# Seven buffers instead of four for the experts' weights, and half blocks loaded two row blocks to a buffer

## The chip, the cores and the metric

The kernel runs on one core of one Trainium2 chip. The metric is the device time of one execution in microseconds (us); the time before is 2666.2 us, the median of 3 runs (2665.56 to 2667.45). Everything is float32.

## What is computed

Three transformer blocks run one after the other on a sequence of 256 tokens of width 1024. Nearly all of the change's effect lies in the mixture of experts that ends the second block. Cut to what matters:

```python
N_EXPERTS, TOP_K, D_EXPERT = 8, 2, 3584        # D_MODEL = 1024, 256 tokens

def swiglu(x, w_in, w_out):
    gate, up = jnp.split(x @ w_in, 2, axis=-1)
    return (jax.nn.silu(gate) * up) @ w_out

def moe_swiglu(x, w_router, w_in, w_out):      # w_in [8, 1024, 7168], w_out [8, 3584, 1024]
    xt = x.reshape(b * s, d)
    logits = (xt @ w_router).astype(jnp.float32)
    top_val, top_idx = lax.top_k(logits, TOP_K)
    top_w = jax.nn.softmax(top_val, axis=-1)
    gates = jnp.sum(jax.nn.one_hot(top_idx, N_EXPERTS) * top_w[..., None], axis=1)
    y = jnp.zeros_like(xt)
    for e in range(N_EXPERTS):
        y = y + gates[:, e:e + 1] * swiglu(xt, w_in[e], w_out[e])
    return y.reshape(b, s, d)
```

An expert has 29.4 MB of `w_in` and 14.7 MB of `w_out`, the eight together 352 MB, and every byte is read once.

## The kernel before

The program is written with tiles from pools. A scheduler turns it into one fixed order of instructions for each engine and adds the waits; on the chip every engine takes its instructions in that order. A tile takes a free buffer of its pool, and whoever writes a buffer anew waits until the last reader of the tile before has done. Two pools matter here, both with buffers of 8 KB in each of the 128 partitions, which is 1 MB: `raw` with 4 buffers, which holds weights as they come from memory, and `big` with 12 buffers (tag `u8`, taken through `K.u8`), which holds activations and operands.

The mixture of experts is in `moe`. The tokens of each expert are picked with matmuls, in groups of 32 tokens: the experts are ranked by how many tokens they got, five have room for 96 tokens (3 groups) and three for 64 (2 groups). They run in four pairs, `PAIRS = [(0, 5), (1, 6), (2, 7), (3, 4)]`; the document calls them pairs 0 to 3. In pairs 0 to 2 a 96-token expert goes with a 64-token one, in pair 3 both have 96. Each expert of a pair is a generator (`run`, and in it `expert`), and the two are stepped in turn, a piece of weights each, after the first of the pair has had `LEAD = 4` pieces alone. The first accumulates in the PSUM pool `mm`, the second in `ps`, so `mm<-wr` and `ps<-wr` tell the two apart in the profile.

In `expert` the hidden width 3584 goes in blocks of 1024: three full blocks and a half block of 512. In the first expert, the first 512 are computed otherwise (`dense`, all tokens, through `linear`), so it has three full blocks and no half block. For a block of `w` columns, 8 row blocks of `w_in` come one after the other (128 rows, gate and up: 1 MB for a full block, 512 KB for a half one), each in a `wr` tile of `raw` (L964 to L966). For each group of tokens four matmuls read the piece (L969), each with 32 columns of weights (the tokens) and the piece as moving data. After the eighth, `silu` and the product are made (L977, L978), and two pieces later `flush` turns the result with transposes (L947) into the tiles `eh` (L949), which lie in `big`. Then 14 pieces of `w_out`, 256 rows and 1 MB each, come into `wr` (L985, L986) and are read by L990. At the end the groups are joined (L1178, L1180), split, and added to the result with the matmuls at L1189.

All loads of weights are issued by SyncE (SP), in the order of the program. SP waits there, with everything behind it, until the `raw` buffer of the next piece is free:

```python
self.raw = pool("raw", 4)
...
raw = k.raw.tile([128, 2048], F32, name="wr")[:, :2 * w].rearrange("p (g n) -> p g n", g=2)
src = w_in[c * 128:c * 128 + 128].rearrange("p (g n) -> p g n", g=2)[:, :, c0:c0 + w]
k.mark = nc.sync.dma_start(raw, src)
```

While the experts run, `big` holds the result `moe_y`, the tokens `xth` and `xtl`, the picked tokens `xg` of the pair and from its second block on those of the next, and two tiles `eh` for each of the two experts: nine buffers of twelve.

Of the kernel before, what the change touches and what calls it, by code (L numbers as in the profile page):

```python
# [10 lines left out]
F32 = mybir.dt.float32  # L11
# [13 lines left out]
class K:  # L25


    def __init__(self, tc, ctx, inp):
        self.tc, self.nc, self.inp = tc, tc.nc, inp
        pool = lambda name, bufs, **kw: ctx.enter_context(tc.tile_pool(name=name, bufs=bufs, **kw))  # L30
        self.raw = pool("raw", 4)
        self.wh = pool("wh", 4)
        self.wl = pool("wl", 4)
        self.big = pool("big", 12)
        self.work = pool("work", 1)
        self.small = pool("small", 3)
        self.const = pool("const", 1)
        self.mm = pool("mm", 3, space=PSUM)
        self.ps = pool("ps", 5, space=PSUM)
        self.consts = {}  # L40
        self.mark = None
        self.pend = []

    def const_in(self, name, queue=None):
        if name not in self.consts:
            src = self.inp["c_" + name]
            t = self.const.tile(list(src.shape), F32, name="c_" + name)
            if queue is not None:
                queue.dma_start(t, src)
            else:  # L50
                self.load(t, src)
            self.consts[name] = t
        return self.consts[name]
# [869 lines left out]
def expert(k, pool, xg, o, cap, w_in, w_out, hidden, evac, first=None, midway=None):  # L923

    nc = k.nc
    ident = k.const_in("ident")
    groups = cap // 32  # L930
    n = hidden // 128
    hs = [k.u8(F32, "eh")[:, :16 * cap].rearrange("p (c t) -> p c t", c=16) for _ in range(2)]
    half = 12 if first else 16
    hidden_units = lambda c, m=1: hs[c >= half][:, c - half * (c >= half):c - half * (c >= half) + m]
    if first:
        first(hidden_units(0, 4))

    def accumulators():
        name = "mm" if pool is k.mm else "ps"
        return [pool.tile([128, 512], F32, name=name) for _ in range(groups)]  # L940

    def turn(g, h, c0, sub):

        m = sub // 128
        p = k.ps.tile([128, m, 64], F32, name="ps")
        for c in range(m):
            nc.tensor.transpose(p[:, c], h[0:64, c * 128:c * 128 + 128], ident[0:64, 0:64])  # L947
        dst = hidden_units(c0 // 128, 2 * m)[:, :, g * 32:g * 32 + 32].rearrange("p (s c) t -> p c s t", s=2)
        nc.vector.tensor_copy(dst, p.rearrange("p c (s t) -> p c s t", s=2))  # L949

    pend = []

    def flush():
        for f in pend:
            f()
        pend.clear()

    starts = list(range(512 if first else 0, hidden, 1024))
    for c0 in starts:
        w = min(1024, hidden - c0)  # L960
        sub = w // 2
        acc = accumulators()
        for c in range(8):
            raw = k.raw.tile([128, 2048], F32, name="wr")[:, :2 * w].rearrange("p (g n) -> p g n", g=2)  # L964
            src = w_in[c * 128:c * 128 + 128].rearrange("p (g n) -> p g n", g=2)[:, :, c0:c0 + w]
            k.mark = nc.sync.dma_start(raw, src)  # L966
            for g in range(groups):
                for j in range(4):
                    nc.tensor.matmul(acc[g][32 * j:32 * j + 32, :sub], xg[:, c, o + 32 * g:o + 32 * g + 32],  # L969
                                     raw[:, j // 2, j % 2 * sub:j % 2 * sub + sub], start=(c == 0), stop=(c == 7),  # L970
                                     tile_position=(0, 32 * j), skip_group_check=True)
            if c == 1:
                flush()
            if c == 7:
                for g in range(groups):
                    h = k.wl.tile([128, 1024], F32, name="wl")[:, :512]
                    nc.scalar.activation(h[64:128, :sub], acc[g][0:64, :sub], AF.Silu)  # L977
                    nc.vector.tensor_tensor(h[0:64, :sub], h[64:128, :sub], acc[g][64:128, :sub], op=OP.mult)  # L978
                    pend.append(partial(turn, g, h, c0, sub))
                if midway and c0 == starts[1]:  # L980
                    midway()
            yield
    acc = accumulators()
    for i in range(0, n, 2):
        raw = k.raw.tile([128, 2048], F32, name="wr").rearrange("p (g n) -> p g n", g=2)  # L985
        k.mark = nc.sync.dma_start(raw, w_out[i * 128:i * 128 + 256].rearrange("(g p) n -> p g n", p=128))  # L986
        for g in range(groups):
            for j in range(4):
                c = i + j // 2
                nc.tensor.matmul(acc[g][32 * j:32 * j + 32], hidden_units(c)[:, 0, 32 * g:32 * g + 32],  # L990
                                 raw[:, j // 2, j % 2 * 512:j % 2 * 512 + 512], start=(i == 0), stop=(i == n - 2),
                                 tile_position=(0, 32 * j), skip_group_check=True)
        if i == 2:
            flush()
        if i < n - 2:
            yield
    for g in range(groups):
        evac(g, acc[g])
    yield


def moe(k, x, xs, w_router, w_in, w_out, y, before_rest):
# [167 lines left out]
    def run(pool, xg, o, cap, wi, wo, pt, g, last, first=None, midway=None):  # L1170
        made = []

        def evac(i, p):
            if not made:
                made.append(k.w(4, [2, 512], F32, "res"))
            res = made[0]
            odd = k.wh.tile([128, 1024], F32, name="wh")[:, :512]
            nc.scalar.copy(odd[:64], p[64:128])  # L1178
            for c in range(2):
                nc.vector.tensor_tensor(res[32 * i:32 * i + 32, c], odd[32 * c:32 * c + 32], p[32 * c:32 * c + 32], op=OP.add)  # L1180

        yield from expert(k, pool, xg, o, cap, wi, wo, hidden, evac, first, midway)
        f = [v.tile([128, 1024], F32R, name=m).rearrange("p (c n) -> p c n", c=2) for v, m in ((k.wh, "wh"), (k.wl, "wl"))]
        k.split(f[0][:cap], f[1][:cap], made[0][:cap])
        for c in range(2):
            for t in range(2):
                q = k.ps.tile([128, 512], F32, name="ps")
                for i in range(2):
                    nc.tensor.matmul(q, pt[:cap, t], f[i][:cap, c], start=(i == 0), stop=(i == 1))  # L1189
                o = slice(c * 512, c * 512 + 512)  # L1190
                nc.vector.scalar_tensor_tensor(y[:, t, o], q, g(t), y[:, t, o], op0=OP.mult, op1=OP.add)
                if last:
                    nc.vector.bn_stats(stats[:, t, c], y[:, t, o])
# [456 lines left out]
```

## Time and profile before

| what | us |
|---|---|
| time, median of 3 runs | 2666.2 |
| the profiled execution's own time | 2663.86 |
| its span (first to last instruction in the trace) | 2662.1 |
| granted TensorE clock over the span | 0.981 |
| PE busy (94% of the span) | 2509.5 |
| DVE busy (45%) | 1187.8 |
| ACT busy (32%) | 855.5 |

The experts' pieces are issued from 1386 us on, and the last matmuls on them end at 2383 us. In the page's 40 slices (66.6 us each) the DMA engines are busy 80% of the time or more from 1464 to 2329 us and move 321 to 401 GB/s there, against 55 to 269 GB/s in the slices before. So the kernel has two regimes: a first one in which DVE and ACT prepare the weights for PE and the DMA has time to spare, and the experts, in which DVE and ACT hardly work, and PE and the DMA are both near their limits. An engine's busy time is the time covered by its instructions; a matmul's end is modelled, so that the last one before a pause counts about 0.2 us more than its slot in a dense row.

### The profile page before, as it was taken

How to read it: one execution, taken by the hardware profiler on the slowest of the kernel's cores; microseconds unless marked ns; L12 is line 12 of the kernel's file. 1: busy time of each engine (PE TensorE's matmuls, PEld its weight loads, DVE VectorE, ACT ScalarE, POOL GpSimd, SP SyncE). 2: the span in 40 equal slices, each digit the busy share in tenths (PEclk: the TensorE clock that was granted, in tenths of full speed). 3: DMA queues.
4: the chain of work that ended last, by engine and by line, in shares of the span. 5: the costliest groups of instructions: out<-in, count | busy, mean ns of one | idle time of the engine just before them, and what ended most of it. 6: DMA issues, size and time to landing. Idle time of an engine off the chain costs nothing. (4 is left out here: it accounts for less than half of the span.)

```text
span 2662.1 us, 40466 instructions
## 1 busy us (share of the span) xinstructions
PE 2509.5 (94%) x16925; PEld 1655.0 (62%) x16925; DVE 1187.8 (45%) x1932; ACT 855.5 (32%) x1291; POOL 60.6 (2%) x82
## 2 busy tenths in 40 slices
PE   8999999999999999999999988988898899888999
PEld 7888888878787887787974322232223233326777
DVE  4555758775555566655472102110211111128665
ACT  4434445444443334443561000000110000005553
POOL 0000000000000000000000000000000000002100
PEclk9999989999999999999999999999999999998999
DMA  7555514453556854556527999999899989877513
GB/s 254 178 173 185 173 55 162 161 188 127 191 181 207 213 174 158 185 185 201 161 96 269 384 358 354 401 339 389 334 375 335 397 340 371 321 289 236 196 64 111
DMA packets 254398, 630.46 MB, mean 237 GB/s; under 512 B 21359, under 2 KB 40064, under 8 KB 253952
## 3 DMA queue, kind: packets, MB, share of 16 engines
q1 hardware_dynamic: 252000, 624.57, 65.3%
q10 hardware_dynamic: 2208, 3.21, 0.9%
q8 instruction: 136, 2.23, 0.3%
q14 instruction: 54, 0.44, 0.0%
HBM read 623.55 MB, written 4.19 MB: 236 GB/s over the span
## 5 line engine op out<-in xcount | busy, mean ns | idle before, releaser
L93 DVE TENSOR_TENSOR wl<-wr,wh 128x1024 fp32r<-128x1024 f32 x494 | 595.0, 1212 | 381.3 <-ACT wh L92 362.8
L92 ACT CAST wh<-wr 128x1024 fp32r<-128x1024 f32 x494 | 512.2, 1044 | 512.8 <-PE mm L164 376.1
L161 PE MATMUL mm<-wh,xh 128*128 128x512 f32 (+2 forms) x1264 | 491.2, 389 | 9.0 <-ACT xh L92 6.4
L164 PE MATMUL mm<-wh,xl 128*128 128x512 f32 (+2 forms) x1264 | 487.1, 386 | 5.9 <-DVE xl L93 5.9
L162 PE MATMUL mm<-wl,xh 128*128 128x512 f32 (+2 forms) x1264 | 485.6, 385 | 2.4 <-DVE wl L93 2.3
L969 PE MATMUL mm<-wr,xg 128*32 128x512 f32 (+1 forms) x2880 | 316.1, 563 | 27.9 <-DMA wr<-moe_w_in 27.6
L161 PEld LDWEIGHTS mm<-wh,xh 128*128 128x128 f32 x1264 | 240.5, 190 | 57.0 <-ACT xh L92 9.9
L164 PEld LDWEIGHTS mm<-wh,xl 128*128 128x128 f32 x1264 | 240.3, 190 | 53.9 <-DVE xl L93 9.6
L162 PEld LDWEIGHTS mm<-wl,xh 128*128 128x128 f32 x1264 | 240.1, 190 | 50.1 <-DVE wl L93 6.6
L969 PE MATMUL ps<-wr,xg 128*32 128x512 f32 (+1 forms) x2304 | 249.8, 543 | 13.0 <-DMA wr<-moe_w_in 12.7
L969 PEld LDWEIGHTS mm<-wr,xg 128*32 128x32 f32 x2880 | 89.5, 111 | 220.4 <-issue 142.8
L990 PE MATMUL mm<-wr,eh 128*32 128x512 f32 x1344 | 164.4, 624 | 34.5 <-DMA wr<-moe_w_out 34.1
L189 PE MATMUL mm<-xh,wh 128*128 128x256 f32 x648 | 185.6, 287 | 2.3 <-ACT wh L92 1.5
L191 PE MATMUL mm<-xh,wl 128*128 128x256 f32 x648 | 185.7, 287 | 1.4 <-DVE wl L93 1.4
L190 PE MATMUL mm<-xl,wh 128*128 128x256 f32 x648 | 185.2, 286 | 0.4 <-DVE xl L93 0.4
L969 PEld LDWEIGHTS ps<-wr,xg 128*32 128x32 f32 x2304 | 71.1, 110 | 151.6 <-issue 96.2
L978 DVE TENSOR_TENSOR wl<-wl,mm 64x512 f32<-64x512 f32 (+1 forms) x45 | 28.6, 637 | 255.9 <-ACT wl L977 255.4
L977 ACT ACTIVATE wl<-mm 64x512 f32<-64x512 f32 (+1 forms) x45 | 24.6, 546 | 349.2 <-PE mm L969 348.9
L990 PE MATMUL ps<-wr,eh 128*32 128x512 f32 x1008 | 123.7, 596 | 6.2 <-DMA wr<-moe_w_out 6.2
L990 PEld LDWEIGHTS mm<-wr,eh 128*32 128x32 f32 x1344 | 41.3, 113 | 138.7 <-issue 82.3
L189 PEld LDWEIGHTS mm<-xh,wh 128*128 128x128 f32 x648 | 125.3, 193 | 3.3 <-ACT wh L92 1.7
L191 PEld LDWEIGHTS mm<-xh,wl 128*128 128x128 f32 x648 | 125.2, 193 | 2.3 <-DVE wl L93 2.3
(469 smaller groups left out, 2656.2 us busy)
## 6 DMA issues: line engine op xcount, KB each, us to landing
wr<-moe_w_in SPq DMA_DIRECT2D x196, 1024.0 KB, 7.3
wr<-moe_w_out SPq DMA_DIRECT2D x112, 1024.0 KB, 7.3
wr<-ffn_w_in SPq DMA_DIRECT2D x66, 1024.0 KB, 5.2
wr<-w_in SPq DMA_DIRECT2D x50, 1024.0 KB, 5.1
wr<-ffn_w_out SPq DMA_DIRECT2D x30, 1024.0 KB, 5.1
wr<-moe_w_in SPq DMA_DIRECT2D x56, 512.0 KB, 6.0
wr<-ret_w_in SPq DMA_DIRECT2D x24, 1024.0 KB, 5.4
wr<-w_mkv SPq DMA_DIRECT2D x8, 1024.0 KB, 5.0
```

The lines of the kernel that those rows point to most:

```text
L92: self.nc.scalar.copy(H, src)
L93: self.nc.vector.tensor_tensor(L, src, H, op=OP.subtract)
L161: nc.tensor.matmul(p, h, wh[:, c:c + m], start=first, stop=False)
L162: nc.tensor.matmul(p, h, wl[:, c:c + m], start=False, stop=False)
L164: nc.tensor.matmul(acc[t][i][:rows, :m], l, wh[:, c:c + m], start=False, stop=last)
L189: nc.tensor.matmul(o, wh[:, s], h, start=first, stop=False, skip_group_check=True)
L190: nc.tensor.matmul(o, wh[:, s], l, start=False, stop=False, skip_group_check=True)
L191: nc.tensor.matmul(o, wl[:, s], h, start=False, stop=(k == kn - 1), skip_group_check=True)
L969: nc.tensor.matmul(acc[g][32 * j:32 * j + 32, :sub], xg[:, c, o + 32 * g:o + 32 * g + 32], raw[:, j // 2, j % 2 * sub:j % 2 * sub + sub], ...
L977: nc.scalar.activation(h[64:128, :sub], acc[g][0:64, :sub], AF.Silu)
L978: nc.vector.tensor_tensor(h[0:64, :sub], h[64:128, :sub], acc[g][64:128, :sub], op=OP.mult)
L990: nc.tensor.matmul(acc[g][32 * j:32 * j + 32], hidden_units(c)[:, 0, 32 * g:32 * g + 32], raw[:, j // 2, j % 2 * 512:j % 2 * 512 + 512], s ...
```

## The change

It counts the experts' pieces. Of every seven, four take a `raw` buffer as before and three take a buffer of `big`. In a half block a buffer takes two row blocks (two transfers of 512 KB, side by side in the 1 MB), and the matmuls on both follow at that one step: a half block has 4 steps instead of 8. Nothing else changes; the arithmetic and its order in each accumulator stay.

```diff
+        self.pieces = 0
...
+    def piece():
+
+        k.pieces += 1
+        if k.pieces % 7 < 4:
+            return k.raw.tile([128, 2048], F32, name="wr")
+        return k.u8(F32, "wr")
+
...
-        for c in range(8):
-            raw = k.raw.tile([128, 2048], F32, name="wr")[:, :2 * w].rearrange("p (g n) -> p g n", g=2)
-            src = w_in[c * 128:c * 128 + 128].rearrange("p (g n) -> p g n", g=2)[:, :, c0:c0 + w]
-            k.mark = nc.sync.dma_start(raw, src)
+        per = 1024 // w
+        for c in range(0, 8, per):
+            raw = piece().rearrange("p (k g n) -> p k g n", k=per, g=2)
+            for i in range(per):
+                src = w_in[(c + i) * 128:(c + i) * 128 + 128].rearrange("p (g n) -> p g n", g=2)[:, :, c0:c0 + w]
+                k.mark = nc.sync.dma_start(raw[:, i], src)
             for g in range(groups):
-                for j in range(4):
-                    nc.tensor.matmul(acc[g][32 * j:32 * j + 32, :sub], xg[:, c, o + 32 * g:o + 32 * g + 32],
-                                     raw[:, j // 2, j % 2 * sub:j % 2 * sub + sub], start=(c == 0), stop=(c == 7),
-                                     tile_position=(0, 32 * j), skip_group_check=True)
-            if c == 1:
+                for i in range(per):
+                    for j in range(4):
+                        nc.tensor.matmul(acc[g][32 * j:32 * j + 32, :sub], xg[:, c + i, o + 32 * g:o + 32 * g + 32],
+                                         raw[:, i, j // 2, j % 2 * sub:j % 2 * sub + sub], start=(c + i == 0), stop=(c + i == 7),
+                                         tile_position=(0, 32 * j), skip_group_check=True)
+            if c + per == 2:
                 flush()
-            if c == 7:
+            if c + per == 8:
...
-        raw = k.raw.tile([128, 2048], F32, name="wr").rearrange("p (g n) -> p g n", g=2)
+        raw = piece().rearrange("p (g n) -> p g n", g=2)
```

Where it moves instructions is seen in three places. The first is SP at the start of the experts: the issues of the first pieces (`wr_11760` is the first of them), the loads of registers (`number`, `more`), and the semaphores that each waits for. Before:

```order
L966 DMA wr_11760<-moe_w_in_2 128x2x1024 [waits DMAHW5_49,DVE_49]
L966 DMA wr_11774<-moe_w_in_2 128x2x1024 [waits DMAHW2_49,DMAHW6_49,DVE_49,Activation_49]
L966 DMA wr_11788<-moe_w_in_2 128x2x1024 [waits DMAHW7_49,DMAHW3_49,DVE_49]
L966 DMA wr_11802<-moe_w_in_2 128x2x1024 [waits DMAHW4_49,DMAHW0_49,DVE_49]
L1209 TENSOR_LOAD number_11503 [waits DVE_49]
L1209 ISA x2
L1238 TENSOR_LOAD more_11518 [waits DVE_49]
L1238 ISA x2
L1238 TENSOR_LOAD more_11518 [waits DVE_49]
L1238 ISA x2
L966 ISA
L966 DMA wr_11830<-moe_w_in_2 128x2x1024 [waits DMAHW1_49,PE_49]
```

With the change:

```order
L976 DMA wr_11788<-moe_w_in_2 128x2x1024 [waits DMAHW7_49,DMAHW3_49,DVE_49]
L1249 TENSOR_LOAD more_11518 [waits DVE_49]
L1249 ISA x2
L1249 TENSOR_LOAD more_11518 [waits DVE_49]
L1249 ISA x2
L976 DMA wr_11802<-moe_w_in_2 128x2x1024 [waits DMAHW4_49,PE_49]
L1220 TENSOR_LOAD number_11503
L1220 ISA x2
L976 ISA
L976 DMA wr_11830<-moe_w_in_2 128x2x1024 [waits PE_49]
L976 DMA wr_11840<-moe_w_in_2 128x2x1024 [waits PE_49]
```

The fourth piece now stands behind the loads of `more`, and it and the two after it take buffers of `big`, whose last readers were matmuls of the attention before. The second place is SP in the half block of pair 0, where the 64-token expert's `w_in` alternates with the other's `w_out`. Before:

```order
L986 DMA wr<-moe_w_out 128x2x1024
L966 ISA
L966 DMA wr<-moe_w_in 128x2x512
L986 DMA wr<-moe_w_out 128x2x1024
L966 ISA
L966 DMA wr<-moe_w_in 128x2x512
```

With the change:

```order
L976 ISA
L976 DMA wr<-moe_w_in 128x2x512
L976 ISA
L976 DMA wr<-moe_w_in 128x2x512
L997 DMA wr<-moe_w_out 128x2x1024 x2
L976 ISA
L976 DMA wr<-moe_w_in 128x2x512
L976 ISA
L976 DMA wr<-moe_w_in 128x2x512
```

The number of transfers stays, and two of 512 KB now follow one another into one buffer. The third place is PE at the change from pair 2 to pair 3, where L1189 (L1200 with the change) adds the last expert of a pair to the result. Before:

```order
L990 MATMUL ps<-wr,eh 32x512 x15
L969 MATMUL mm<-wr,xg 32x512 x5
L1189 MATMUL ps<-wh,pback 128x512 x4
L969 MATMUL mm<-wr,xg 32x512 x4
L1189 MATMUL ps<-wl,pback 128x512 x4
L969 MATMUL mm<-wr,xg 32x512 x39
```

With the change:

```order
L1001 MATMUL ps<-wr,eh 32x512 x15
L980 MATMUL mm<-wr,xg 32x512 x5
L1200 MATMUL ps<-wh,pback 128x512 x4
L980 MATMUL mm<-wr,xg 32x512 x4
L1200 MATMUL ps<-wl,pback 128x512 x4
L980 MATMUL mm<-wr,xg 32x512 x39
```

Nothing moved there.

## Rows read from the trace of the kernel before

**Rows 1.** Windows: at the experts' first matmuls, the four pairs, and all after

```profile
core 0: us, PE busy (x) PEld busy (x) DVE busy (x) ACT busy (x) POOL busy (x), PEclk, DMA share, GB/s
1411.00:1427.00 16.00, 16.00 (x100) 10.29 (x102) 3.68 (x10) 1.71 (x3) 0.00 (x0) 1.00 0.24 87
...
1425.00:1645.00 220.00, 194.97 (x1734) 59.15 (x1726) 25.87 (x46) 15.36 (x29) 0.00 (x0) 0.98 0.97 371
1645.00:1887.00 242.00, 211.68 (x1972) 66.22 (x1972) 36.85 (x64) 19.48 (x35) 0.00 (x0) 0.99 0.97 372
1887.00:2133.00 246.00, 216.19 (x1962) 67.61 (x1962) 34.40 (x60) 18.47 (x34) 0.00 (x0) 0.97 0.94 359
2133.00:2383.00 250.00, 241.54 (x2298) 82.00 (x2298) 36.61 (x66) 16.72 (x31) 0.00 (x0) 0.97 0.92 347
2383.00:2662.00 279.00, 253.52 (x1361) 202.00 (x1360) 188.20 (x395) 139.38 (x250) 25.93 (x27) 0.95 0.44 145
```

**Rows 2.** DMA issues of the page: tile, KB each, median us to landing

```profile
wr<-moe_w_in SPq DMA_DIRECT2D x196, 1024.0 KB, 7.3
wr<-moe_w_out SPq DMA_DIRECT2D x112, 1024.0 KB, 7.3
...
wr<-moe_w_in SPq DMA_DIRECT2D x56, 512.0 KB, 6.0
```

**Rows 3.** DMA packets in two stretches of pair 0, 1440 to 1500 and 1500 to 1520

```profile
DMA packets 6321, 24.42 MB, mean 407 GB/s; under 512 B 373, under 2 KB 373, under 8 KB 6316
...
DMA packets 1915, 7.39 MB, mean 369 GB/s; under 512 B 115, under 2 KB 115, under 8 KB 1914
...
wr<-moe_w_in SPq DMA_DIRECT2D x7, 1024.0 KB, 6.3
```

**Rows 4.** Waits of SP's queue from 1425 to 2383: total us, times, longest

```profile
SPq L966 <- PE mm L969: 228.0, 90, 12.6
SPq L986 <- PE mm L990: 148.6, 55, 5.4
SPq L966 <- PE ps L969: 112.9, 91, 2.8
```

**Rows 5.** Timeline of PE in pair 0 and in pair 3

```profile
1463.32 1.92 PE L969 MATMUL ps<-wr,xg 128*32 128x512 f32 x16
1465.86 2.78 PE L969 MATMUL mm<-wr,xg 128*32 128x512 f32 x24 [0.62 <-DMA wr<-moe_w_in]
1468.46 1.90 PE L969 MATMUL ps<-wr,xg 128*32 128x512 f32 x16
...
2179.59 2.76 PE L969 MATMUL mm<-wr,xg 128*32 128x512 f32 x24
2182.17 2.76 PE L969 MATMUL ps<-wr,xg 128*32 128x512 f32 x24
2184.74 2.76 PE L969 MATMUL mm<-wr,xg 128*32 128x512 f32 x24
```

**Rows 6.** Windows around the half blocks of pairs 0 to 3

```profile
1555.00:1610.00 55.00, 45.66 (x440) 14.37 (x432) 3.47 (x8) 1.93 (x4) 0.00 (x0) 0.91 0.88 325
1780.00:1810.00 30.00, 23.75 (x310) 9.97 (x306) 4.28 (x10) 2.30 (x5) 0.00 (x0) 0.94 0.88 307
2020.00:2055.00 35.00, 27.84 (x340) 11.50 (x335) 4.28 (x10) 2.30 (x5) 0.00 (x0) 0.90 0.86 301
2260.00:2310.00 50.00, 44.08 (x574) 19.36 (x564) 6.51 (x16) 3.33 (x8) 0.00 (x0) 0.97 0.84 289
```

**Rows 7.** Windows around the changes of pair

```profile
1645.00:1660.00 15.00, 13.19 (x102) 4.38 (x106) 6.39 (x9) 1.60 (x2) 0.00 (x0) 1.00 0.78 298
1887.00:1905.00 18.00, 17.73 (x108) 5.76 (x112) 3.94 (x5) 0.21 (x1) 0.00 (x0) 0.72 0.54 195
2125.00:2145.00 20.00, 17.04 (x102) 5.50 (x102) 8.12 (x12) 2.21 (x3) 0.00 (x0) 0.74 0.57 208
```

**Rows 8.** Waits of PE, first from 1425 to 2133, then from 2133 to 2383

```profile
PE mm L990 <- DMA wr<-moe_w_out: 30.9, 33, 3.7
PE mm L969 <- DMA wr<-moe_w_in: 26.8, 40, 1.2
PE ps L969 <- DMA wr<-moe_w_in: 9.4, 10, 2.5
PE ps L1189 <- ACT wh L92: 7.6, 5, 3.0
...
PE ps L1189 <- ACT wh L92: 3.8, 2, 3.0
PE ps L969 <- DMA wr<-moe_w_in: 3.2, 2, 2.9
PE mm L990 <- DMA wr<-moe_w_out: 3.2, 2, 1.6
PE mm L969 <- DMA wr<-moe_w_in: 0.8, 1, 0.8
```

**Rows 9.** Timeline of PE after a half block, and at the change to pair 3

```profile
1598.19 5.35 PE L990 MATMUL mm<-wr,eh 128*32 128x512 f32 x24 [3.68 <-DMA wr<-moe_w_out]
...
2133.11 2.07 PE L1189 MATMUL ps<-wh,pback 64*128 64x512 f32 x4 [2.96 <-ACT wh L92]
```

## The prediction

> **What bounds the kernel now.** I read the windows first, cut at the pairs of experts. In pairs 0 to 2, 1425 to 2133 us, the DMA brings 371, 372 and 359 GB/s, and PE idles 25.0, 30.3 and 29.8 us; in pair 3 the DMA brings 347 GB/s and PE idles only 8.5 us of 250 [rows 1]. The reader is to see two engines, each near its limit, that take turns in waiting for the other.
>
> What the DMA can do stands in the packets: 407 GB/s over 60 us of pair 0, but 369 GB/s from 1500 to 1520, although every transfer there is a full 1 MB [rows 3]. So one piece of 1.049 MB needs 1.049 / 0.407 = 2.58 us, and something else than its size holds the rate down at 1500. The waits of SP's queue say what: its longest are for PE's matmuls L969 and L990, the readers of the buffers, 228.0 and 148.6 us in total [rows 4]. From issue to landing a piece takes 7.3 us in the median [rows 2]. With four buffers one comes round every 4 x 2.58 = 10.3 us, which leaves 3.0 us for PE to use the piece and for SP to issue the next. Matmuls on one piece take just that long.
>
> What PE can do stands in the timeline: 24 records (12 matmuls) of a 96-token expert start every 2.57 us in pair 3. A 64-token expert's 16 records take two thirds, 1.72 us. In pair 0 two pieces come in 5.12 us (1465.86 to 1470.98), and PE waits for both [rows 5]. So in pairs 0 to 2 PE needs 4.3 us for two pieces and the DMA 5.16: the DMA bounds, if it is kept fed. In pair 3 PE needs 5.14, with turns on top: PE bounds.
>
> **The change, part by part.** All sums are against the profiled execution's own 2663.9 us, 2.3 below the median of 2666.2; the same gain is taken off that median.
>
> *Pairs 0 to 2, the buffers and the merged halves together.* The bytes of the three are 0.371 x 220 + 0.372 x 242 + 0.359 x 246 = 259.9 MB [rows 1]. At 407 GB/s they take 639 us instead of 708, so 69 us are lost to an empty queue. Of these, three places can be told apart:
> - Around the half blocks 55 + 30 + 35 = 120 us bring 37.6 MB [rows 6], worth 92 us: 28 lost. A buffer there holds only 512 KB.
> - At the changes of pair, 15 us at 298, 18 at 195 and the first 8 of 20 at 208 GB/s bring 9.6 MB [rows 7], worth 24 of 41 us: 17 lost. PE stands in the end of one pair and frees no buffer.
> - The rest, 547 us with 212.7 MB, is worth 523: 24 lost, as at 1500 [rows 3].
>
> No row shows seven transfers in flight. The rate is 369 GB/s where the queue runs short and 407 where it is full with four [rows 3]; I take 407, the nearer, and no more, and the 369 goes to the rival of no gain. With seven buffers a round is 7 x 2.58 = 18.1 us. Less the 7.3 us to landing, PE may be 10.8 us late with a piece before the queue runs dry, instead of 3.0. A merged half needs two issues, but one buffer for 1 MB. The 28 and the 24 should go: what keeps PE from the pieces inside a pair is short, a turn of one group's result at a time. One of its larger losses there is of the queue's own making: after a wait of 3.68 us for a piece the next 24 records took 5.35 us instead of 2.78 [rows 5, 9], at the lower of the two clocks. At a change of pair PE loses about as much as seven buffers cover: 2.96 us of waiting for ACT's split [rows 9], then eight matmuls for the old pair, and at two of the three changes a mean granted clock of 0.72 over 18 us and 0.74 over 20 [rows 7], which is 10 us at 1.2 GHz. I leave 10 us of the 69 in place: between 0 (all covered) and 17 (the changes of pair cost what they cost today), nearer to the second, since PE's order there is the same before and after. That is a gain of 59.
>
> *The start.* From 1411 to 1427 the DMA brings 87 GB/s, while PE computes the first expert's dense part [rows 1]: four pieces fill the four buffers. Now three more go out, behind two register loads. Three pieces are 7.7 us that pair 0 no longer waits for; nothing, if the loads hold SP to the end of that stretch. I take 7, since PE has work until 1425 and the DMA is the bound after it.
>
> *Pair 3.* PE's waits for pieces are 3.2 + 3.2 + 0.8 = 7.2 us [rows 8]; they can go, but nothing else can, for the DMA needs only 0.347 x 250 / 0.407 = 213 us. The lower end is 0, should the waits move into turns. I take 6.
>
> *What costs nothing.* Three in seven of the pieces lie at other addresses, with the same layout; two issues for one merged half stand where two stood. SP has time for them, since it waits 490 us in the three rows shown alone [rows 4]. The register loads of a pair queue ahead of pieces that are not yet needed. Everything behind 2383 us [rows 1] only moves forward: its first weights wait for a loop that comes after the experts.
>
> **Sum:** 59 + 7 + 6 = 72 us, 2663.9 - 72 = 2591.9; on the median **2594 us**.
>
> **The rivals.**
>
> *The halves stay slow.* The buffer is merged, but a transfer still carries 512 KB. If that, and not the buffer, holds the half blocks at 301 to 325 GB/s [rows 6], their 28 us stay: a gain of 44, 2622 us. For it: the three lowest rates outside the changes of pair are there. Against it: a half lands after 6.0 us, little sooner than the 7.3 of a full one [rows 2], as if it stood in the same queue, and 369 GB/s occur without any half. The Trainium skill has the same as a rule (DMA: Bandwidth & Descriptors, Measured): transfers of 1 MiB and more for 75% of the peak. An estimate from its peak of 435 GB/s is 326, close to the 325 of the first window; no run yet shows which of the two reasons it is.
>
> *Both engines reach their limits.* Nothing is lost at the changes either: the 10 us left above go too, and 3 more in pair 3, the rest of its 7.2 and 1.5 for a slow stretch behind the waits (50 us at 0.97 [rows 6]). Gain 72 + 10 + 3 = 85, 2581 us. PE's busy time in pairs 0 to 2, 622.8 us [rows 1], lies below the DMA's 639, which allows it; that they must both be busy at once speaks against it.
>
> *No gain.* It has two ways, and in both the time stays near 2666 us. The change may not do what it says: if `big` has no three buffers free, its pieces wait for operands and the depth stays near four. By count nine of twelve are in use, so three are free, and the order shows the first pieces there waiting for matmuls of the stage before, long done. Or the memory does not hold 407 GB/s for long: the pairs stand at 347 to 372 GB/s [rows 1], and 407 lasted 60 us [rows 3]. Against it: nothing wears off in those 60 us, and the lower means have stretches of 195 to 325 GB/s in them [rows 6, 7] that explain most of the distance. The Trainium skill gives such a figure (DMA: Bandwidth & Descriptors, Specifications): about 358 GB/s of HBM for one core, by which nothing would be left to gain. The 407 GB/s contradict it here, and the same page (Measured) ties the half share to both cores of a pair streaming; this program runs on one.
>
> *Slower: the operands wait for the pieces.* A tile `eh` or `xg` now often takes a buffer that a piece had, and its first writer waits until that piece has landed and been read. There are 15 such tiles of `eh` and 3 of `xg` after the first ones. If each held PE for more than 72 / 18 = 4.0 us, the gain would be gone; at the full latency of 7.3 us they cost 131, less 72 is 59 more: 2725 us. Against: PE takes its matmuls in order, and the piece is mostly read before the transposes that make the tile; and today DVE's copies wait for PE, hardly PE for them.
>
> **How the numbers follow.** A measurement of this kernel can tell about 0.2%, 5.3 us. The forecast, a gain of 54 to 80, has 0.58; both limits reached 0.16; slow halves, or another partial gain of 25 to 54, 0.14; no gain 0.06; slower 0.06. The range leaves out most of the last two and takes in the partial gains to 32 us and the limits plus 9: **2572 to 2634 us**. Faster by over 0.2%: 0.58 + 0.16 + 0.14 = 0.88; within: 0.06; slower: 0.06.
>
> **What would show it.** Right: pairs 0 to 2 at 395 GB/s or more, PE's waits for `wr` in them down from 67 us [rows 8] to under 35, the landing above 11 us in the median; the windows of the half blocks like the rest; the change to pair 3 still with some 10 us at the lower clock and 3 us of waiting for ACT; pair 3 some 244 us long and bound by PE. Wrong: windows of the half blocks at 325 GB/s and below (the first rival); PE idle before L949's readers or L1131's (the slower one); a rate that stays at 360 to 372 GB/s although SP no longer waits.

## The result, and the profile after

The changed kernel takes 2585.7 us (median of 4 runs, 2585.0 to 2590.1) against 2665.9 us before: a ratio of 0.9705, 95% interval 0.9688 to 0.9722. The forecast was 2594.0. The profiled execution of the change took 2586.28 us with a span of 2584.5, so from profile to profile the gain is 77.6 us.

The windows of the change, cut at the same places of the program as [rows 1] (first matmuls, pairs 0 to 3, all after):

```profile
core 0: us, PE busy (x) PEld busy (x) DVE busy (x) ACT busy (x) POOL busy (x), PEclk, DMA share, GB/s
1411.00:1427.00 16.00, 16.00 (x98) 10.51 (x100) 4.12 (x12) 1.71 (x3) 0.00 (x0) 1.00 0.79 291
...
1425.00:1621.00 196.00, 187.19 (x1738) 60.27 (x1730) 26.35 (x47) 15.09 (x28) 0.00 (x0) 0.99 1.02 402
1621.00:1846.00 225.00, 206.69 (x1972) 69.18 (x1972) 36.70 (x65) 19.64 (x35) 0.00 (x0) 1.00 1.03 407
1846.00:2067.00 221.00, 207.10 (x1962) 69.39 (x1962) 34.32 (x60) 17.98 (x33) 0.00 (x0) 0.98 1.01 397
2067.00:2306.00 239.00, 237.41 (x2298) 79.30 (x2298) 37.21 (x67) 17.32 (x32) 0.00 (x0) 0.99 0.93 358
2306.00:2584.00 278.00, 253.06 (x1360) 201.93 (x1360) 187.57 (x394) 138.87 (x249) 25.81 (x27) 0.95 0.44 146
```

Pairs 0 to 2 go from 708 to 642 us and from 371, 372 and 359 GB/s to 402, 407 and 397: 66 us. Pair 3 goes from 250 to 239: 11 us. What lies behind goes from 279 to 278. In the first window 291 instead of 87 GB/s are loaded, which is 3.3 MB or 8 us of the DMA's time. In pairs 0 to 2 the DMA is now the bound, with one clear gap left, at the second change of pair; in pair 3 PE idles 1.6 us of 239.

The page's 40 slices (64.6 us each), the DMA's busy tenths and its GB/s, show how even that is: of the nine slices wholly inside pairs 0 to 2, the 24th to the 32nd, eight have 401 to 409 GB/s, and the one with the second change of pair has 376:

```profile
DMA  7556423454555854555634999999999999957523
GB/s 261 171 189 192 147 82 124 162 185 159 179 177 204 222 171 140 201 178 174 213 102 157 392 408 406 409 406 404 376 409 401 409 370 388 378 196 259 174 66 114
```

The waits of PE, first from 1425 to 2067, then from 2067 to 2306:

```profile
PE mm L1001 <- DMA wr<-moe_w_out: 23.9, 33, 3.9
PE ps L1200 <- ACT wh L93: 6.8, 5, 3.0
PE mm L980 <- DMA wr<-moe_w_in: 3.5, 6, 0.7
PE ps L1001 <- DMA wr<-moe_w_out: 3.1, 5, 0.8
PE ps L980 <- DMA wr<-moe_w_in: 0.8, 1, 0.8
...
PE ps L1200 <- ACT wh L93: 3.8, 2, 3.0
```

The three long waits for pieces in pairs 0 to 2 were 67 us [rows 8]; all of them are 31.3 now, and pair 3 has none. What PE still waits for in pairs 0 to 2 is a DMA that has no time to spare. No reader of the tiles `eh` (written at L950 in the changed kernel) and no gather of `xg` appears among the waits.

The issues of DMA (tile, KB each, median us to landing) and the waits of SP's queue from 1425 to 2300:

```profile
wr<-moe_w_in SPq DMA_DIRECT2D x196, 1024.0 KB, 12.9
wr<-moe_w_out SPq DMA_DIRECT2D x112, 1024.0 KB, 15.1
...
wr<-moe_w_in SPq DMA_DIRECT2D x56, 512.0 KB, 12.3
```

```profile
SPq L976 <- PE mm L980: 151.9, 45, 13.8
SPq L997 <- PE mm L1001: 85.0, 34, 7.9
SPq L976 <- PE ps L980: 81.0, 38, 8.6
```

A full piece lands 13 to 15 us after its issue instead of 7.3 [rows 2]: it is asked for earlier and stands in the queue, which is what keeps the queue full. SP still waits for PE's readers, now for pieces that PE needs much later.

Last, the half blocks of pairs 0 to 3 and the three changes of pair. The cuts are near those of [rows 6, 7], not the same: the last window begins 5 us ahead of the end of pair 2, the one of [rows 7] 8 us ahead.

```profile
1540.00:1570.00 30.00, 25.88 (x296) 9.43 (x292) 2.98 (x6) 1.93 (x4) 0.00 (x0) 0.94 1.04 401
1731.00:1776.00 45.00, 42.48 (x554) 19.94 (x550) 8.29 (x18) 4.82 (x10) 0.00 (x0) 1.00 1.04 398
1953.00:1998.00 45.00, 41.55 (x546) 19.53 (x542) 8.29 (x18) 4.82 (x10) 0.00 (x0) 1.00 1.04 398
2186.00:2236.00 50.00, 50.00 (x650) 22.30 (x646) 9.73 (x21) 5.67 (x12) 0.00 (x0) 1.00 1.00 380
1621.00:1636.00 15.00, 13.24 (x102) 4.38 (x106) 6.33 (x9) 1.55 (x2) 0.00 (x0) 1.00 1.03 409
1846.00:1864.00 18.00, 17.98 (x124) 5.57 (x128) 3.94 (x5) 0.00 (x0) 0.00 (x0) 0.81 0.81 314
2062.00:2082.00 20.00, 17.04 (x116) 5.17 (x112) 6.66 (x9) 2.21 (x3) 0.00 (x0) 0.83 0.98 391
```

The half blocks of pairs 0 to 2 run at 398 to 401 GB/s instead of 301 to 325 [rows 6]; with the kernel before cut as widely as here (1553 to 1596, 1763 to 1817 and 2007 to 2062) it is 327 to 335. At the changes of pair the first, 409 GB/s, loses nothing any more. The second still dips, from 1856 us on: in the 45 us around it (1831 to 1876) the mean is 362 GB/s, so that at 407 GB/s 45 x (1 - 362/407) = 5.0 us are lost. With the last window 8 us ahead, as in [rows 7], it has 409 GB/s instead of 208; its dip comes later (283 GB/s from 2077 to 2087), in pair 3, where PE is the bound.

### The profile page after: what moved, and what is told of

Its sections match the earlier page's. It is cut to its first block, busy times and chain, and to the rows that moved or that the text cites. A ratio compares the mean times of both kernels' runs of the same rounds, so it can differ in the third digit from the quotient of the medians.

```text
span 2584.5 us, 40384 instructions
## 1 busy us (share of the span) xinstructions
PE 2482.8 (96%) x16925; PEld 1658.1 (64%) x16925; DVE 1188.2 (46%) x1933; ACT 854.9 (33%) x1290; POOL 60.5 (2%) x82
## 5 line engine op out<-in xcount | busy, mean ns | idle before, releaser
L162 PEld LDWEIGHTS mm<-wh,xh 128*128 128x128 f32 x1264 | 240.3, 190 | 57.2 <-ACT xh L93 10.3
L980 PEld LDWEIGHTS mm<-wr,xg 128*32 128x32 f32 x2880 | 95.4, 111 | 183.6 <-issue 161.9
L1001 PE MATMUL mm<-wr,eh 128*32 128x512 f32 x1344 | 157.8, 599 | 24.0 <-DMA wr<-moe_w_out 23.9
L191 PEld LDWEIGHTS mm<-xl,wh 128*128 128x128 f32 x648 | 125.6, 194 | 0.8 <-DVE xl L94 0.6
## 6 DMA issues: line engine op xcount, KB each, us to landing
wr<-moe_w_in SPq DMA_DIRECT2D x196, 1024.0 KB, 12.9
wr<-moe_w_out SPq DMA_DIRECT2D x112, 1024.0 KB, 15.1
```

The costliest lines, as they stand in the source:

```text
L162: nc.tensor.matmul(p, h, wh[:, c:c + m], start=first, stop=False)
L191: nc.tensor.matmul(o, wh[:, s], l, start=False, stop=False, skip_group_check=True)
L980: nc.tensor.matmul(acc[g][32 * j:32 * j + 32, :sub], xg[:, c + i, o + 32 * g:o + 32 * g + 32], raw[:, i, j // 2, j % 2 * sub:j % 2 * sub + ...
```

## The experiments

The theory is the forecast's: the rate is set by how late PE may be with a piece before the queue runs dry, and this allowance grows by 2.58 us, one piece's time, with every buffer. Its rivals were that the size of a transfer sets it, that the half blocks need the merging, or that each transfer more in the queue raises the rate by itself.

To compare the runs, this table cuts each profile at the first matmul on the pieces of each pair, and pair 3 ends with the last matmul of L1200 (L1189 before). The ratio is to the time before on the same chip. The first matmul on a piece stands among those of the dense part and moves from run to run (1414.4 us with five buffers, 1417.3 with six, 1418.9 to 1419.9 in the others), so pair 0 is best compared by the end of pair 2, given in the last column.

| kernel | median us | ratio, 95% | pairs 0 to 2 | pair 3 | end of pair 2 |
|---|---|---|---|---|---|
| before | 2665.9 | | 226.1 + 236.8 + 245.9 = 708.8 | 262.9 | 2128.3 |
| four buffers, merged | 2629.9 | 0.986 (0.984 to 0.989) | 216.5 + 228.3 + 234.7 = 679.5 | 253.6 | 2098.4 |
| five, merged | 2601.0 | 0.975 (0.972 to 0.978) | 210.7 + 222.5 + 228.4 = 661.6 | 252.5 | 2076.0 |
| six, merged | 2590.8 | 0.972 (0.969 to 0.975) | 205.5 + 219.2 + 223.2 = 647.9 | 252.3 | 2065.2 |
| seven, merged (the change) | 2585.7 | 0.9705 (0.9688 to 0.9722) | 201.6 + 219.7 + 221.4 = 642.7 | 250.9 | 2062.6 |
| seven, not merged | 2583.8 | 0.969 (0.966 to 0.972) | 201.7 + 219.2 + 222.3 = 643.2 | 247.4 | 2062.2 |

**Seven buffers, not merged.**

```diff
-        per = 1024 // w
+        per = 1
-            raw = piece().rearrange("p (k g n) -> p k g n", k=per, g=2)
+            raw = piece()[:, :2 * w].rearrange("p (k g n) -> p k g n", k=per, g=2)
```

Expected: 

> Seven buffers, but in a half block each holds 512 KB again (8 steps). Forecast's theory (the round of the buffers decides): in a half block, where 1 MB and 512 KB pieces alternate, a round is 3.5 x 2.58 + 3.5 x 1.29 = 13.5 us, less 7.3 to landing 6.2 us of lateness, twice what four full buffers had; the windows of the half blocks reach 390 GB/s or more and the time is 2586 to 2592 us. Rival (a half block needs the merging, since a buffer with 512 KB is what keeps the queue short): its 28 us come back, windows at 301 to 325 GB/s, 2614 us.

Measured: 2583.8 us (2580.9 to 2585.4), 2 us below the theory's span and far from the rival's 2614. Its half blocks of pairs 0 to 2:

```profile
1539.00:1578.00 39.00, 36.10 (x390) 11.87 (x386) 2.98 (x6) 1.93 (x4) 0.00 (x0) 1.00 1.03 403
1730.00:1775.00 45.00, 43.56 (x558) 18.43 (x554) 8.37 (x18) 4.83 (x10) 0.00 (x0) 1.00 1.03 389
1952.00:1998.00 46.00, 43.16 (x554) 18.28 (x550) 8.38 (x18) 4.83 (x10) 0.00 (x0) 1.00 1.04 397
```

Buffers with 512 KB in them are no handicap when there are seven.

**Four buffers, merged.**

```diff
-        if k.pieces % 7 < 4:
+        if True:
```

Expected: 

> Merged half blocks, but four buffers everywhere. Forecast's theory: a half block then loses what the rest loses, 24 of 523 us or 4.6%, that is 4 of 92 us instead of 28; a gain of 24, 2642 us, its windows at 360 to 390 GB/s, and the changes of pair and the start as before. Rival (at four buffers any half block starves, because two issues into one buffer wait for the same free buffer and its matmuls free 1 MB at once): within 5 us of the time before, 2661 to 2671, windows under 340 GB/s.

Measured: 2629.9 us (2624.4 to 2632.7), 36 us gained in the ratio and 12 us more than the theory had. Its pairs, and the half blocks of pairs 0 and 1:

```profile
1418.90:1635.40 216.50, 196.32 (x1777) 61.16 (x1778) 27.97 (x49) 17.01 (x31) 0.00 (x0) 1.00 0.97 377
1635.40:1863.70 228.30, 207.46 (x1957) 68.31 (x1960) 33.33 (x59) 16.92 (x31) 0.00 (x0) 1.00 1.00 386
1863.70:2098.40 234.70, 211.39 (x1969) 68.30 (x1964) 34.31 (x60) 18.32 (x33) 0.00 (x0) 0.98 0.98 377
2098.40:2352.00 253.60, 244.48 (x2325) 83.96 (x2318) 45.32 (x78) 20.52 (x35) 0.00 (x0) 0.97 0.93 349
1553.00:1580.00 27.00, 23.99 (x280) 8.67 (x277) 2.98 (x6) 1.93 (x4) 0.00 (x0) 1.00 1.04 400
1753.00:1799.00 46.00, 40.75 (x526) 18.94 (x522) 8.28 (x18) 4.82 (x10) 0.00 (x0) 1.00 1.03 394
```

That is a miss: 2642 was expected. Pairs 0 to 2 gain 29.3 us, the whole of what the half blocks had lost (28), not all but 4 of it: with whole buffers the half blocks run at 391 to 400 GB/s, with transfers of 512 KB still. The other 9.3 us are pair 3's, whose half block ran at 289 GB/s [rows 6] and which the expectation had forgotten: it took 58 us before (2254 to 2312, 630 matmuls) and takes 49 here (2225 to 2274, 642 matmuls). So either part of the change cures the half blocks alone, and the two gains do not add: merging gives 36 us (by the ratio) to 39 (by the table's cuts) with four buffers and nothing with seven. Merging also changes the order, since two half pieces of one expert now follow one another; no run with four buffers separates this from the bytes in a buffer.

**Five buffers, and six** (`k.pieces % 5 < 4`, `k.pieces % 6 < 4`, with merging).

Expected of five: 

> The change with five buffers (one of every five pieces in the operands' pool). Forecast's theory: the round is 12.9 us, less 7.3 is 5.6 us of lateness instead of 3.0, enough for a turn or a slow stretch inside a pair but not for a change of pair: of the 80 us gained, 52 inside the pairs come back nearly whole, 2.6 of the start's 8, some 6 of pair 3's 11, and 3 of the 12 at the changes; 2600 to 2610 us. Rival (each transfer more in the queue raises the rate alike): a third of the gain, 2639 us.

Expected of six: 

> The change with six buffers (two of every six pieces in the operands' pool). Forecast's theory: a round of 15.5 us, 8.2 us of lateness; all inside the pairs, 5 of the start's 8, most of pair 3, and half of the changes: 2589 to 2596 us. Rival (each transfer more in the queue raises the rate alike): two thirds of the gain, 2612 us.

Measured: 2601.0 us (2598.1 to 2604.4) and 2590.8 us (2590.0 to 2594.7), both in the theory's spans and far from the rival's 2639 and 2612. (These spans were set when the gain with seven was known.) From merged four on, the medians gain 29, 10 and 5 us, and the end of pair 2 comes 22.4, 10.8 and 2.6 us earlier; by the ratios the last step is 3 us, which their intervals do not separate. Each buffer covers a rarer lateness.

The change from pair 1 to pair 2 shows it at one place. These are the first 10 us from the first matmul of L1200 (L1189 before) there, in the kernel before, with four, five and six buffers merged, and with the change:

```profile
1887.27:1897.27 10.00, 10.00 (x36) 3.50 (x40) 3.92 (x5) 0.00 (x0) 0.00 (x0) 0.50 0.26 86
1868.56:1878.56 10.00, 10.00 (x40) 3.61 (x44) 3.93 (x5) 0.00 (x0) 0.00 (x0) 0.53 0.27 90
1852.44:1862.44 10.00, 10.00 (x36) 3.39 (x40) 3.92 (x5) 0.00 (x0) 0.00 (x0) 0.51 0.37 122
1846.84:1856.84 10.00, 10.00 (x52) 3.35 (x56) 3.92 (x5) 0.00 (x0) 0.00 (x0) 0.66 0.52 193
1846.02:1856.02 10.00, 10.00 (x52) 3.38 (x56) 3.92 (x5) 0.00 (x0) 0.00 (x0) 0.66 1.03 409
```

PE is late with the pieces there, and the DMA keeps going for longer with every buffer. The clock (0.50 to 0.66) is not what makes the difference: the run in the next experiment, with seven buffers at this place, has 407 GB/s at 0.50. Nor is it that four transfers in the queue cannot reach the rate: with four buffers 407 GB/s were held for 60 us [rows 3]. The landing of a full `w_in` piece grows by 1.7 to 2.1 us a buffer. The issue row of five:

```profile
wr<-moe_w_in SPq DMA_DIRECT2D x196, 1024.0 KB, 9.0
```

and of six:

```profile
wr<-moe_w_in SPq DMA_DIRECT2D x196, 1024.0 KB, 10.8
```

The queue is longer with every buffer, but where it no longer runs dry its length buys nothing.

**The start with four buffers.**

```diff
-        if k.pieces % 7 < 4:
+        if k.pieces <= 10 or k.pieces % 7 < 4:
```

Expected: 

> The change, but the first ten pieces all in raw, so that four and not seven are loaded while the dense part of the first expert runs; seven buffers from the eleventh piece on. Forecast's theory (three pieces of 2.58 us that pair 0 no longer waits for): 7 to 8 us slower than the change, 2593 us, pair 0 longer by that and the other pairs the same. Rival (the start is made good later, since PE catches up with what it has): within 3 us of the change, 2583 to 2589.

Measured: 2590.9 us (2587.1 to 2598.1), ratio 0.9721 (0.9694 to 0.9749), which is 4 to 5 us above the change's and not told apart from it by these runs; the theory had 7 to 8, the rival at most 3. In the profile the first window brings 113 GB/s, and pair 0 takes 209.9 us instead of 201.6, which is 8.3; pairs 1 to 3 are within 1.2 us. The profiled execution was the slowest of the four, so the start is worth between 4 and 8 us; the forecast's 7 lies in it.

**Every piece in two transfers of 512 KB.**

```diff
-                k.mark = nc.sync.dma_start(raw[:, i], src)
+                nc.sync.dma_start(raw[:, i, 0], src[:, 0])
+                k.mark = nc.sync.dma_start(raw[:, i, 1], src[:, 1])
...
-        k.mark = nc.sync.dma_start(raw, w_out[i * 128:i * 128 + 256].rearrange("(g p) n -> p g n", p=128))
+        nc.sync.dma_start(raw[:, 0], w_out[i * 128:i * 128 + 128])
+        k.mark = nc.sync.dma_start(raw[:, 1], w_out[i * 128 + 128:i * 128 + 256])
```

(The half blocks keep their transfers, which have 512 KB already.) Expected: 

> The change with every piece of 1 MB loaded in two transfers of 512 KB (w_in: gate, then up; w_out: one row block, then the other), so twice the issues on SP, with the same bytes and buffers. Theory (the buffers' round and not the transfer's size sets the rate): pairs 0 to 2 stay at 395 to 407 GB/s, 2583 to 2592 us. Rival of the forecast (transfers of 512 KB do not reach the rate): pairs 0 to 2 at 325 GB/s or a little above, 642 x 402 / 325 = 794 us instead of 642, 2738 us.

Measured: 2584.1 us (2579.6 to 2586.4). Its pairs 0 to 2:

```profile
1418.80:1619.90 201.10, 199.65 (x1772) 72.00 (x1771) 26.75 (x48) 15.29 (x29) 0.00 (x0) 1.00 1.02 401
1619.90:1841.00 221.10, 218.07 (x1961) 79.98 (x1960) 33.70 (x60) 17.43 (x33) 0.00 (x0) 1.00 1.03 405
1841.00:2062.40 221.40, 217.81 (x1970) 80.11 (x1966) 33.45 (x60) 17.72 (x33) 0.00 (x0) 0.98 1.01 397
```

and its issues:

```profile
wr<-moe_w_in SPq DMA_DIRECT2D x440, 512.0 KB, 10.2
wr<-moe_w_out SPq DMA_DIRECT2D x224, 512.0 KB, 10.2
```

664 transfers of 512 KB run at the rate of 304 of 1 MB and 56 of 512 KB (four pieces of the dense part stay whole), and the rival's 2738 us are far off. The size of a transfer is not what held the half blocks down. The Trainium skill's rule of 1 MiB for 75% of the peak (DMA: Bandwidth & Descriptors, Measured), given there for loads issued by GpSimd, does not hold here for SP's queue with several transfers in it: 397 to 405 GB/s with 512 KB stand well above the 326 that the prediction worked out from it.

**Other order of the experts.** One thing is left: pairs 0 to 2 are bound by the DMA, pair 3 by PE. To spread PE's work, the five experts with 96 tokens run one after the other in `mm` and the three with 64 beside them in `ps`, with six buffers. The core of the edit (it steps them 202 to 126; the expectation says 206):

```diff
+    streams = [[0, 1, 2, 3, 4], [5, 6, 7]]
...
+    while next(going[0], done) is not done:
+        owed += 126
+        while owed >= 202 and open_b:
+            owed -= 202
+            open_b = next(going[1], done) is not done
```

Expected: 

> Other order of the experts with six buffers: the five experts with 96 tokens run one after the other in mm, the three with 64 in ps, stepped 206 to 126, so that both streams end together and PE's work per piece is 2.25 us everywhere instead of 2.15 in pairs 0 to 2 and 2.57 in pair 3; each expert has its own gathered tokens. Theory (pair 3 is bound by PE, the rest by DMA, and only pair 3's 29 us above 85.6 MB / 407 GB/s are left to gain): the rate stays near 400 GB/s over all eight experts, 850 to 870 us from the first piece's matmul to the last result instead of 894, 2555 to 2570 us. Rival (where both engines are near their limits each loses what the other makes it wait): 2580 to 2592 us, no gain over six buffers at 2591.

Measured: 2583.6 us (2574.3 to 2587.9), a miss, and inside the rival's span: beside the change this is no difference that these runs can tell. The next runs were measured beside the change on one chip. Since each expert's gathered tokens fit a buffer of 4 KB in the `work` pool, the mixed order can have seven and eight buffers for weights:

```diff
-        xg = k.u8(F32, "xg")[:, :8 * n].rearrange("p (c n) -> p c n", c=8)
+        xg = k.w(4, [8, n], F32, "xg")
...
-        if k.pieces % 6 < 4:
+        if k.pieces % 7 < 4:
```

Expected of the change itself: 

> The changed kernel once more, as the measure on the same chip for the runs beside it. Every theory: 0.970 to 0.972 of the time before, 2583 to 2592 us.

Of seven buffers without merging: 

> Seven buffers without merging, beside the change itself on the same chip. Theory (with seven buffers the round of a half block is long enough either way): within 0.2% of the change, 5 us. Rival (merging still gives a part of its 39 us): over 5 us slower than the change.

Of the mixed order with seven: 

> The mixed order of the experts with the gathered tokens in the work pool, which leaves room for seven buffers. Theory (only the distribution of PE's work held pair 3): 2.6 us off the start against six buffers and nothing lost at the turns of both streams at once; 8 to 20 us faster than the change, 2565 to 2577 us. Rival (what one engine loses, the other does not make good): within 5 us of the change.

Of the mixed order with eight (`k.pieces % 8 < 4`): 

> The same with eight buffers (four of every eight pieces in the operands' pool). Theory: one more piece of 2.6 us at the start, and the rest already at the DMA's rate with seven: 0 to 4 us faster than the mixed order with seven. Rival (each buffer more still raises the rate): over 8 us faster than with seven.

| kernel | median us of 6 runs | lowest to highest | ratio, 95% |
|---|---|---|---|
| the change | 2586.2 | 2583.8 to 2589.1 | 0.9704 (0.9672 to 0.9736) |
| seven, not merged | 2582.5 | 2577.7 to 2585.6 | 0.9686 (0.9653 to 0.9718) |
| mixed order, seven | 2575.0 | 2571.8 to 2576.4 | 0.9658 (0.9627 to 0.9690) |
| mixed order, eight | 2574.6 | 2570.4 to 2578.5 | 0.9656 (0.9624 to 0.9687) |

The mixed order with seven buffers is 11 us faster than the change, inside its theory's span, and no run of it is as slow as a run of the change; an eighth buffer adds nothing that these runs can tell. That the order alone gives the 11 us is not shown, since the gathered tokens lie in another pool too. Leaving out the merging costs nothing, as expected; if anything it gains 4 us, which is within the 5 that a measurement tells. With seven buffers the mixed order brings 390 to 408 GB/s in each stretch of 100 us from 1500 to 2200. Its first and last windows with the experts:

```profile
1425.00:1500.00 75.00, 75.00 (x669) 25.96 (x664) 9.44 (x19) 7.29 (x15) 0.00 (x0) 1.00 0.92 349
...
2200.00:2290.00 90.00, 81.25 (x826) 26.69 (x822) 10.43 (x21) 6.33 (x12) 0.00 (x0) 1.00 0.97 380
```

From the first piece's matmul to the last result it takes 874.8 us (1424.0 to 2298.8) instead of 893.6, 19 us less, of the 29 that pair 3 had above the DMA's time; 8 go again, 4 at the later first piece and 4 behind the experts (275.1 instead of 271.0 us). What stays is the first 75 us, where PE has no pause at all and the DMA stands at 349 GB/s.

## Why the prediction was right, point by point

**Pairs 0 to 2, forecast 59 + 7.** Measured 66 us, from 708 to 642. The mechanism is shown by the row of buffers: five and six came inside the spans that the lateness gave them, and at the change to pair 2 the DMA kept going for longer with each buffer. Four, merged, did not: it was 12 us faster than expected. The sizes 3.0 and 10.8 us of lateness are not shown by any run: the 7.3 us to landing that the prediction takes off the round grows itself by 1.7 to 2.1 us with every buffer, so it is in part time in the queue. What the runs bear out is the step of 2.58 us a buffer. That 407 GB/s would hold for more than the 60 us in which it had been seen [rows 3] was an assumption; pair 1 now holds 407 over 225 us. The Trainium skill's 358 GB/s for one core (DMA: Bandwidth & Descriptors, Specifications) is no limit in this run of one core.

**The halves, 28 of the 59.** The size was right: merging alone gains 29.3 us in these pairs. That they were put down to the two edits together hid that one is enough. The step "a buffer there holds only 512 KB" fits what four buffers did, with the order of the pieces not separated from it; for seven it could have been worked out ahead that a round of 3.5 x 2.58 + 3.5 x 1.29 = 13.5 us is longer than that of four full ones, 10.3, and that merging then adds nothing.

**The changes of pair, 10 us left in place of 17.** Measured 5. Here the sum left too much: seven buffers cover more of a change of pair than the prediction took. PE still waits 2.96 us for ACT's split and then runs at the lower clock:

```profile
2067.40 1.19 PE L1200 MATMUL ps<-wh,pback 64*128 64x512 f32 x4 [2.96 <-ACT wh L93]
2068.52 1.49 PE L980 MATMUL mm<-wr,xg 128*32 128x512 f32 x8
2069.94 2.07 PE L1200 MATMUL ps<-wl,pback 64*128 64x512 f32 x4
2071.95 8.56 PE L980 MATMUL mm<-wr,xg 128*32 128x512 f32 x60
```

In this execution the slow stretch behind it is shorter. In the row of 2133.11 [rows 9] four matmuls took 2.07 us from the first on; here the first four take 1.19, and 60 on the pieces take 8.56 us, longer than 60 x 2.57 / 24 = 6.4 by 2 us. The mean granted clock over the windows of 18 and 20 us is 0.81 and 0.83 instead of 0.72 and 0.74 [rows 7]: 18 x 0.09 + 20 x 0.09 = 3.4 us of full speed. But the buffers do not ensure it: when the changed kernel was measured again, its third change of pair had the long stretch once more, its first four matmuls 2.07 us, and the DMA kept its rate:

```profile
2056.60:2076.60 20.00, 17.04 (x98) 5.44 (x102) 7.97 (x11) 2.21 (x3) 0.00 (x0) 0.74 1.03 409
```

At the same clock of 0.74 the kernel before had 208 GB/s [rows 7]. So PE was as late there as before, or nearly, and the DMA went on. Inside the pairs some 3 us are lost that the forecast had at nothing (at 407 GB/s, 0.402 x 196 + 0.407 x 225 + 0.397 x 221 = 258.1 MB take 634 us, so 8 of the 642 are lost in all). So of the 69 us that the sum had as lost, 61 came back instead of 59, and in this sum 5 are left for the start instead of 7. That the two meet the measured 66 to the microsecond is luck.

**The start, forecast 7.** The pair's length says 8.3, the medians 4 to 5, and pairs 0 to 2 bring 1.8 MB less than before (258.1 instead of 259.9), which is 4.4 us at 407 GB/s. That the start gains is shown, its size only as 4 to 8.

**Pair 3, forecast 6.** Here the step failed that "they can go, but nothing else can". Measured 11 us, 250 to 239. PE's waits for pieces, 7.2 us [rows 8], went whole. And PE's busy time fell from 241.5 to 237.4 us at a granted clock of 0.99 instead of 0.97 [rows 1]. The clock was low in two places before (2133 to 2143 and 2293 to 2303), in one after (2067 to 2077):

```profile
2133.00:2143.00 10.00, 9.89 (x36) 3.49 (x40) 3.95 (x5) 0.06 (x1) 0.00 (x0) 0.50 0.27 93
2293.00:2303.00 10.00, 8.16 (x82) 3.38 (x78) 1.09 (x4) 0.00 (x0) 0.00 (x0) 0.83 0.79 273
...
2067.00:2077.00 10.00, 9.60 (x48) 3.31 (x52) 3.94 (x5) 0.34 (x1) 0.00 (x0) 0.66 1.03 410
```

Of the 4 us, 10 x (1 - 0.83) = 1.7 are a slow stretch behind a wait for a piece, and go with the wait. Another 10 x (0.66 - 0.50) = 1.6 are the shorter slow stretch at the change of pair, which varies between executions of the same kernel, as said above. The rest is no more than the modelled ends of matmuls before the six waits that are gone can make, 0.2 us each. The sum counted only idle time; the rival of both limits had 1.5 us for the clock behind the waits. By the table's cuts, where pair 3 gains 12.0 us, the run with four merged buffers has 9.3 of them, nearly all in the half block, 58 us before and 49 there.

**The sum.** 66 + 11 + 1 behind = 78 us against 72, within the profile's 77.6. The time lies between the forecast, 2594, and the rival in which both engines reach their limits, 2581. Of that rival's 13 us more, the 3 in pair 3 came, and 2 beyond them, most of these by the clock at the change of pair; of the 10 at the changes 5 came, but pairs 0 to 2 gave them back elsewhere. The rest of the 8 us between forecast and result is 1 behind the experts and 2 to 3 by which medians and profiled executions differ.

**The other rivals.** Halves that stay slow: fallen, by 398 to 401 GB/s in the half blocks, by the 391 to 400 of four buffers merged, and by the run with 512 KB everywhere. No gain: fallen, since the landing of 12.9 us shows the deeper queue and the memory holds the rate. Operands that wait for pieces: in the list of PE's waits above no transpose of L948 stands at all, so its price here is nothing that the profile shows.

**A reading.** The prediction has PE waiting for both of two pieces in pair 0. Its rows [rows 5] show one wait of 0.62 us for the two, before the piece of the 96-token expert; no term of the sum uses it.

## What to carry to other kernels

A loop that streams weights needs enough buffers that their round, counted in time per piece, outlasts the time to landing plus the reader's lateness; each further buffer covers one piece's time more (2.58 us here) and brings less (here 29, 10 and 3 to 5 us). Do not take the time to landing as fixed: it grows with the queue. Two edits that cure the same stall don't add up: price each alone before crediting both. When waits go away, PE's busy time can fall as well, since a slow stretch behind a wait goes with it (1.7 us in pair 3). Once the queue is full, the next gain may lie in spreading the work so that both engines are evenly loaded in every stretch (11 us here, together with the other place of the gathered tokens).

## What was not expected of the hardware

The core's DMA engines held 407 GB/s over the 225 us of pair 1, and splitting each 1 MB into two transfers changed neither that rate (405) nor the time (2584.1 us) by more than these runs can tell: with a full queue the number of transfers cost nothing that could be measured. In that run a piece of 512 KB lands after 10.2 us in the median, less than the 12.9 to 15.1 us of the pieces of 1 MB, although there are seven buffers of 1 MB in both.

After the same wait of 2.96 us at a change of pair, the mean granted clock of the 20 us around it was not the same from run to run: 0.83 and 0.83 in the change, 0.83 and 0.74 when it was measured again, 0.74 and 1.00 with seven buffers not merged. A difference of some us between two single profiles can be this alone.
